# Split weights that begin at places of their own in SBUF: one change to a two-layer encoder kernel

## The chip, the cores and the metric

The kernel runs on one core of one Trainium2 chip. The metric is the device time of one execution in microseconds (us), lower is better. A core has five engines that run side by side: PE (TensorE, matrix products; its weight loads are shown apart, as PEld), ACT (ScalarE), DVE (VectorE), POOL (GpSimd) and SP (SyncE, here only a queue for DMA transfers). SBUF, the working memory, has 128 partitions; PSUM takes the products.

## What is computed

The reference is an encoder of two layers on a sequence of 256 tokens with 1024 features, in float32. Each layer is a mixer and a feed-forward part:

```python
def mixer_sublayer(x, ...):
    proj = rms_norm(x, n1) @ w_in_l                  # 1024 -> 2560
    out_a = neighbourhood_attention(...)             # 4 heads
    out_d = dilated_window_attention(...)            # 6 heads
    out_c = gqa_block_attention(...)                 # 6 heads on 2 key heads
    mix = concat(rms_norm(out_a), rms_norm(out_d), rms_norm(out_c))
    return x + mix @ w_out_l                         # 1024 -> 1024

def channel_sublayer(x, n2, w_gu, cw, cb, w_dn):
    g, u = split(rms_norm(x, n2) @ w_gu)             # 1024 -> 2 x 2816
    g = depthwise_conv_centred(g, cw, cb)            # three taps along the tokens
    return x + (gelu(g) * u) @ w_dn                  # 2816 -> 1024
```

Nearly all the arithmetic is in the four products with weights (w_in, w_out, w_gate_up, w_down).

## The kernel before, in words

**Split products.** PE reads float32 operands in a form of reduced precision (float32r), so each float32 value is split in two: hi is the value cast to float32r, lo is the rest. A product is made of three: hi by hi, hi by lo and lo by hi (`mm3`, lines 708 to 711). The activations are split once into tiles (hT, mixT_hi and mixT_lo, ch and cl), the weights on the way in.

**Units.** The weights come in units of at most 2048 float32 values per partition (8192 bytes), listed by `units_of` in the order of use. A layer has 51 (`PER_LAYER`): 12 units of the input projection, 6 of the output projection (together `LAST_OUT` = 18), then 33 of the feed-forward part in the order of `FFN`. There the 11 steps each have a gate unit G, an up unit U and a down unit D. For each unit, `load` (line 644) starts a DMA transfer into one of four raw buffers, and `split` (line 676) makes hi and lo from it piece by piece: ACT casts raw into hi (the CAST of `wp_hi<-wp_raw` in the profile), DVE subtracts (the TENSOR_TENSOR of `wp_lo<-wp_raw,wp_hi`). hi and lo have two buffers each, `wp_hi` and `wp_lo`, so two units are split at any time: PE reads one while ACT and DVE write the other. `unit` (line 697) hands out the next one.

**Which operand a unit is.** In the projections and in the down products the split weights are the moving operand, streamed through PE in 256, 384 or 512 columns, and the activations are the stationary one, 128 columns loaded by a LDWEIGHTS ahead of each matmul. In the gate and up products (`half_up`, line 1337) it is the other way round: the weights are loaded, 128 columns at a time, and h2 (in the buffer hT) is streamed. A gate or up unit is two halves of 8 wide matmuls (512 columns, hi of the weights by hi and lo of h2 at once) and 8 narrow ones (256 columns, lo of the weights). A down unit is 24 matmuls of 512 columns.

**Kept units.** The 6 output-projection units of the second layer are loaded and split early, during the first layer's feed-forward part, and kept in DRAM (`keep`, line 628). Four of them come back into hi and lo by DMA from POOL's queue (the `nc.gpsimd.dma_start` in `split`); the last two have tiles of their own (kc and qc).

**Where tiles lie.** Tiles stand one behind the other in SBUF in the order of their allocation. Two tiles ahead of the wp pool, `minus_half` and `few_out`, are wider than what is used of them, and the raw, hi and lo buffers, hT, ch, cl, mixT and the other operands of matmuls begin on multiples of 512 bytes within the partition. Exceptions are const_x, which lies 384 bytes past one, and every second slice of heads in the value tiles const_v, 256 bytes past one.

**The order of the work.** Calls on `nc` are recorded as operations, and `Plan.order` (line 323) sets their order by a model of the engines' times; the table `PLACES` (line 229) shifts some by hand. `emit` (line 467) writes them out, so all instructions carry its line 472 in the profile, and groups are told apart by their tiles.

Of the kernel before, what the change touches and what calls it, by code (L numbers as in the profile page):

```python
# [12 lines left out]
F32R = mybir.dt.float32r  # L13
# [5 lines left out]
P = 128  # L19
S = 256  # L20
NT = S // P
D = 1024
# [14 lines left out]
UNIT = 2048  # L37
# [4 lines left out]
RAWS, PARTS, AHEAD, CHUNK = 4, 2, 2, 512  # L42
# [34 lines left out]
FFN = [("G", 0), ("U", 0)]  # L77
# [161 lines left out]
class Plan:  # L239
# [5 lines left out]
    def pool(self, real, name, bufs, space=bass.MemoryType.SB):  # L245
        return PlanPool(self, real, name, bufs, space)
# [271 lines left out]
def encoder_kernel(  # L518
# [26 lines left out]
    wp = pool("wp", 3)  # L545
# [78 lines left out]
    PER_LAYER = len(views) // DEPTH  # L624
    LAST_OUT = PER_LAYER - len(FFN)
# [18 lines left out]
    def load(i):  # L644
# [28 lines left out]
                nc.sync.dma_start(rv[:, c:e], v[:, c:e])  # L673
        raws.append(raw)

    def split(i):
        v = views[i]
        a, b = v.shape[1], v.shape[2]
        n = a * b
        raw = raws[i]  # L680
        if isinstance(raw, list):
            parts.append(raw)
            return
        hi = wp.tile([P, UNIT], F32R, tag="hi", name=f"hi{i}", bufs=PARTS)
        lo = wp.tile([P, UNIT], F32R, tag="lo", name=f"lo{i}", bufs=PARTS)
        h = b if i < 2 else b * max(1, CHUNK // b)
        if i in kept:
            for d, z in zip(kept[i], (hi, lo)):
                nc.gpsimd.dma_start(z[:, :n], d)
        for c in range(0, n if i not in kept else 0, h):  # L690
            e = min(c + h, n)
            nc.scalar.copy(hi[:, c:e], raw[:, c:e])
            nc.vector.tensor_tensor(lo[:, c:e], raw[:, c:e], hi[:, c:e].bitcast(F32), op=ALU.subtract)
        r = lambda z: z[:, :n].rearrange("p (a b) -> p a b", b=b)
        parts.append((r(hi), r(lo)))

    def unit():

        i = taken[0]
        taken[0] += 1  # L700
        with nc.later(SPLIT_LATER):
            while len(raws) < min(i + AHEAD + RAWS - PARTS, len(views)):
                load(len(raws))
            while len(parts) < min(i + AHEAD, len(views)):
                split(len(parts))
        return parts[i]
# [182 lines left out]
    for l in range(DEPTH):  # L889
# [3 lines left out]
        if l == 0:  # L893
            gains_T(0, 1)
            split(0)
# [656 lines left out]
```

## Time and profile before

| | |
|---|---|
| time, median of 3 runs | 605.8 us (604.55 to 605.87) |
| time of the profiled execution | 605.52 us |
| its span, first to last instruction | 603.7 us |
| PE busy | 598.0 us (99%) |
| PEld busy | 526.5 us (87%) |
| DVE busy | 485.0 us (80%) |
| ACT busy | 428.6 us (71%) |
| POOL busy | 81.0 us (13%) |
| DMA | 121.44 MB, 201 GB/s over the span |

Of the 605.52 us, 1.8 lie around the span. Busy time is the union of an engine's instructions. A matmul's recorded duration includes a modelled tail that overlaps the next one, so PE's pace is read from starts: the length of a piece of the chain of waits divided by its matmuls. The mean granted clock of PE over the span is 1.000 of full speed.

### The profile page before, as it was taken

What the parts mean: (1) busy time and instruction counts of PE and PEld (TensorE: products, weight loads), DVE (VectorE), ACT (ScalarE), POOL (GpSimd) and SP (SyncE); (2) the same over time, 40 slices, a digit from 0 to 9 for tenths busy, and PEclk for the clock granted to TensorE, in tenths of its full rate; (3) what the DMA queues carried; (4) which work ended last, traced back from release to release, by engine and by line L of the source; (5) the groups of instructions that cost most, each with busy time, mean ns of one, the idle gap of its engine ahead of it and who ended that gap; (6) DMA issues with size and microseconds to landing.
All of it is one profiled execution on the core that took longest, in us unless ns stands there. A gap on an engine that the chain in (4) does not pass through costs nothing.

```text
span 603.7 us, 9899 instructions
## 1 busy us (share of the span) xinstructions
PE 598.0 (99%) x3496; PEld 526.5 (87%) x3496; DVE 485.0 (80%) x995; ACT 428.6 (71%) x1065; POOL 81.0 (13%) x130
## 2 busy tenths in 40 slices
PE   8999999999999999999999999999999999999997
PEld 7999898888888888888899989888888888888886
DVE  4899988997788988888777898777977777777775
ACT  6889999696566767666688899676766556665661
POOL 2733030102400000000023214421000000000000
PEclk9999999999999999999999999999999999999999
DMA  8993313567588898989454726844465556555601
GB/s 281 292 334 108 106 36 108 181 202 241 174 239 295 280 347 301 331 291 318 153 148 157 254 71 244 280 177 140 140 208 203 171 186 210 175 178 206 197 12 69
DMA packets 85217, 121.44 MB, mean 201 GB/s; under 512 B 9880, under 2 KB 69880, under 8 KB 85168
## 3 DMA queue, kind: packets, MB, share of 16 engines
q1 hardware_dynamic: 82896, 112.17, 55.9%
q0 software_dynamic: 1728, 8.39, 4.1%
q8 instruction: 27, 0.44, 0.3%
q10 hardware_dynamic: 544, 0.26, 0.2%
q14 instruction: 22, 0.18, 0.1%
HBM read 110.93 MB, written 9.88 MB: 200 GB/s over the span
## 4 chain that ended last, share of the span: by engine, by line
PE 97%; ACT 1%; DVE 1%; POOL 0%; issue 0%; DVEq 0%; POOLq 0%
PE psw_w L472 53%; PE psa_a L472 44%; ACT act_s2k L472 0%; POOL small_rstd L472 0%; ACT act_z L472 0%; DVE act_z L472 0%; ACT act_hT L472 0%; DVE wp_lo L472 0%; DVE act_sw L472 0%; POOL small_ms L472 0%; DVE const_x L472 0%; DVE act_qo L472 0%; ACT wp_hi L472 0%; POOL const_warm L472 0%; DVEq L472 0%
## 5 line engine op out<-in xcount | busy, mean ns | idle before, releaser
L472 DVE TENSOR_TENSOR wp_lo<-wp_raw,wp_hi 128x512 fp32r<-128x512 f32 (+2 forms) x332 | 231.4, 731 | 57.2 <-ACT wp_hi L472 40.3
L472 ACT CAST wp_hi<-wp_raw 128x512 fp32r<-128x512 f32 (+2 forms) x332 | 203.0, 663 | 21.6 <-PE psw_w L472 10.1
L472 PE MATMUL psw_w<-act_hT,wp_hi 128*128 128x512 f32 x704 | 179.8, 393 | 0.0
L472 PEld LDWEIGHTS psw_w<-act_hT,wp_hi 128*128 128x128 f32 x704 | 127.8, 189 | 24.2 <-DVE act_hT L472 0.6
L472 PE MATMUL psa_a<-wp_hi,act_hT 128*128 128x384 f32 (+2 forms) x448 | 112.9, 332 | 0.7 <-ACT wp_hi L472 0.7
L472 PEld LDWEIGHTS psw_w<-act_hT,wp_lo 128*128 128x128 f32 x704 | 97.7, 190 | 6.7
L472 PE MATMUL psw_w<-act_hT,wp_lo 128*128 128x256 f32 x704 | 102.2, 282 | 0.0
L472 PEld LDWEIGHTS psa_a<-wp_hi,act_hT 128*128 128x128 f32 x448 | 78.4, 189 | 3.3 <-ACT wp_hi L472 0.9
L472 PE MATMUL psa_a<-wp_lo,act_hT 128*128 128x384 f32 (+2 forms) x224 | 74.4, 334 | 0.1
L472 ACT COPY act_s2k<-psw_w 128x256 f32<-128x256 f32 x88 | 32.4, 372 | 59.4 <-PE psw_w L472 58.9
L472 PE MATMUL psa_a<-wp_lo,act_ch 128*128 128x512 f32 (+1 forms) x176 | 68.3, 388 | 0.0
L472 PE MATMUL psa_a<-wp_hi,act_ch 128*128 128x512 f32 x176 | 68.2, 388 | 0.0
L472 PE MATMUL psa_a<-wp_hi,act_cl 128*128 128x512 f32 (+1 forms) x176 | 67.5, 387 | 0.0
L472 DVE TENSOR_TENSOR act_s2k<-psw_w,act_s2k 128x256 f32<-128x256 f32 x88 | 36.6, 421 | 12.8 <-ACT act_s2k L472 12.0
L472 PEld LDWEIGHTS psa_a<-wp_lo,act_hT 128*128 128x128 f32 x224 | 42.3, 189 | 2.4 <-DVE wp_lo L472 1.1
L472 PEld LDWEIGHTS psa_a<-wp_hi,act_cl 128*128 128x128 f32 x176 | 33.1, 188 | 6.8
L472 PEld LDWEIGHTS psa_a<-wp_hi,act_ch 128*128 128x128 f32 x176 | 33.1, 188 | 6.3
L472 PEld LDWEIGHTS psa_a<-wp_lo,act_ch 128*128 128x128 f32 x176 | 33.1, 188 | 6.0
L472 DVE SCALAR_TENSOR_TENSOR act_s2k<-act_s2k,act_cw,act_s2k 128x255 f32<-128x255 f32 x88 | 36.8, 477 | 1.4 <-ACT act_s2k L472 1.3
L472 ACT ACTIVATE act_s2k<-act_s2k 128x512 f32<-128x512 f32 x22 | 13.9, 632 | 30.3 <-DVE act_s2k L472 30.2
L472 ACT ACTIVATE act_s2k<-act_s2k,act_cw 128x256 f32<-128x256 f32 x44 | 24.1, 596 | 15.3 <-DVE act_s2k L472 15.3
L472 POOL TENSOR_TENSOR small_rstd<-small_ms,const_mh 128x6 f32<-128x6 f32 (+2 forms) x26 | 30.9, 1188 | 14.2 <-DVE small_ms L472 12.6
(132 smaller groups left out, 792.0 us busy)
## 6 DMA issues: line engine op xcount, KB each, us to landing
wp_raw<-in_w_gate_up_dram SPq DMA_DIRECT2D x44, 1024.0 KB, 4.9
wp_raw<-in_w_down_dram SPq DMA_DIRECT2D x22, 1024.0 KB, 7.2
wp_raw<-in_w_in_dram SPq DMA_DIRECT2D x14, 768.0 KB, 5.2
wp_raw<-in_w_in_dram SPq DMA_DIRECT2D x8, 1024.0 KB, 6.8
wp_raw<-in_w_out_dram SPq DMA_DIRECT2D x8, 768.0 KB, 9.3
dram_khi<-act_mixT_hi SPq DMA_DIRECT2D x4, 768.0 KB, 3.6
dram_klo<-act_mixT_lo SPq DMA_DIRECT2D x4, 768.0 KB, 8.3
wp_lo<-dram_klo POOLq DMA_DIRECT2D x4, 768.0 KB, 4.7
```

The source lines that it names most:

```text
L472: getattr(o.engine.real, o.method)(*map(real, o.args), **{k: real(v) for k, v in o.kw.items()})
```

## The change: a place for each unit

Each hi and lo tile grows from 8192 to 8704 bytes per partition, and the unit begins in it at an offset that a table gives, in bytes, for hi and for lo. The table has a row for the 12 units of the input projection (the 6 of the output projection take its first six pairs again), one for the steps of the gate and up units, and one for the steps of the down units. The same offsets hold in both layers. All are multiples of 16. Everything that writes or reads the unit (cast, subtraction, kept transfer, matmul) uses the shifted place. The instructions on every engine and their order are the same as before. Later tiles move up by up to 2048 bytes in all, in steps of 512, and so keep their remainder.

```diff
+    APART = {
+        "w": [(0, 64), (64, 0), (32, 32), (192, 192), (448, 448), (256, 256), (0, 192), (320, 64), (16, 16), (96, 96), (480, 480), (352, 352)],
+        "G": [(0, 64), (16, 16), (48, 48), (64, 96), (96, 80), (128, 32), (256, 192), (288, 224), (352, 320), (416, 448), (480, 480)],
+        "D": [(0, 0), (64, 64), (0, 64), (64, 0), (192, 192), (192, 0), (320, 320), (448, 448), (256, 256), (0, 256), (16, 16)],
+    }
+
+    def places_of(i):
+
+        n = i % PER_LAYER - LAST_OUT
+        if n < 0:
+            return APART["w"][(n + LAST_OUT) % 12]
+        kind, s = FFN[n]
+        return APART["D" if kind == "D" else "G"][s]
+
     def split(i):
...
-        hi = wp.tile([P, UNIT], F32R, tag="hi", name=f"hi{i}", bufs=PARTS)
-        lo = wp.tile([P, UNIT], F32R, tag="lo", name=f"lo{i}", bufs=PARTS)
+        hi, lo = (
+            wp.tile([P, UNIT + 128], F32R, tag=g, name=f"{g}{i}", bufs=PARTS)[:, at // 4 : at // 4 + UNIT]
+            for g, at in zip(("hi", "lo"), places_of(i))
+        )
```

## The prediction

> **What bounds the kernel now.** I read the page's busy times first, then its chain of waits, then who waits for whom on PE, and then the chain again inside one stretch of the feed-forward part.
>
> ```profile
> span 603.7 us, 9899 instructions
> PE 598.0 (99%) x3496; PEld 526.5 (87%) x3496; DVE 485.0 (80%) x995; ACT 428.6 (71%) x1065; POOL 81.0 (13%) x130
> PE 97%; ACT 1%; DVE 1%; POOL 0%; issue 0%; DVEq 0%; POOLq 0%
> PE psw_w L472 <- POOL const_warm L472: 1.0, 1, 1.0
> PE psa_a L472 <- ACT wp_hi L472: 0.7, 1, 0.7
> ```
>
> PE is busy for 598.0 of 603.7 us, 97% of the chain that ends last is PE itself, and the waits on PE add up to 1.7 us. So the time is the sum of 3496 start-to-start distances on PE. No other engine sets it: what a change does to the time is what it does to those distances, unless it makes PE wait for something that it doesn't wait for now.
>
> The next rows are the chain between 138 and 172 us (start, length, matmuls in the piece). A piece `psa_a x24` is one down unit (24 matmuls of 512 columns); a piece `psw_w x64` is an up unit and the next gate unit (32 matmuls of 512 columns on hi, 32 of 256 on lo).
>
> ```profile
> 138.31 5.47 PE psa_a L472 x24
> 143.77 11.15 PE psw_w L472 x64
> 154.92 5.47 PE psa_a L472 x24
> 160.38 11.15 PE psw_w L472 x64
> ```
>
> The pieces repeat to 0.01 us, although they use other buffers and other steps. From them: 5.47 / 24 = 227.9 ns per 512-column matmul. In the piece of 64, 32 x 227.9 ns = 7.29 us, which leaves 3.86 us for the 32 narrow ones, 120.5 ns each. The 256 columns between the two cost 107.4 ns, 0.42 ns a column; 512 columns at that rate are 214.8 ns, and 13.1 ns are left over in each matmul whatever its width. This constant is the only thing in a matmul that a change of address could touch, since width, count and order stay.
>
> How far a single matmul strays from its usual length is in the rows of the tiles wp_hi and wp_lo (duration min/median/max, count):
>
> ```profile
> L472 PEld LDWEIGHTS psw_w<-act_hT,wp_hi x704: 186/188/192, 120.1 to 587.1; 128*128 128x128 f32 x176
> L472 PE MATMUL psw_w<-act_hT,wp_hi x704: 387/389/497, 120.1 to 587.3; 128*128 128x512 f32 x176
> L472 PE MATMUL psw_w<-act_hT,wp_lo x704: 274/283/287, 120.4 to 588.4; 128*128 128x256 f32 x176
> L472 PE MATMUL psa_a<-wp_hi,act_mixT_hi x56: 387/393/503, 84.0 to 408.3; 128*128 128x512 f32 x56
> L472 PE MATMUL psa_a<-wp_lo,act_mixT_hi x56: 387/395/506, 84.3 to 408.6; 128*128 128x512 f32 x56
> ```
>
> These durations contain a modelled tail, so only their differences count. A 512-column matmul is 387 ns at least, 389 in the middle, and 393 to 395 in the middle of the output projection; a 256-column one on lo is 274 at least and 283 in the middle, 287 at most. The weight load varies from 186 to 192. So a matmul of one width does vary by some ns, always with hi and lo on multiples of 512 bytes: something in how the weight load and the streaming meet moves it, and it is not excluded that the place of the operands is part of that.
>
> **The change, part by part.** *What is moved.* Every matmul that reads a split unit from the wp pool counts. Counted in the code there are 1408 in the gates and ups, 672 in the projections, 540 in the downs and 168 in the output projections, 2788 in all. By the table of places 328 of these still read from an offset of zero; 2460 read from another (912 of 256 columns, 304 of 384, 1244 of 512). No instruction is added, removed or reordered, and no semaphore changes.
>
> *What 0.3% means.* A measurement of this kernel can tell about 0.3%, 1.8 us, from no change. Over 2460 matmuls that is 0.74 ns each: the whole question is whether the constant of 13.1 ns moves by 0.7 ns on the average over the places.
>
> *Price on PE.* The trace of before holds two groups whose weights do not begin on a multiple of 512 bytes. Adding up the sizes of the tiles in the order of allocation, const_x lies 384 bytes past one, and in const_v every second slice of heads begins 256 past one. Beside them stand transposes from aligned tiles and the aligned narrow matmuls:
>
> ```profile
> L472 PE MATMUL psw_w<-const_ident,const_x x64: 270/272/421, 4.7 to 417.7; 128*128 128x128 f32 x64
> L472 PE MATMUL psw_w<-const_ident,act_z x60: 270/272/273, 28.6 to 379.4; 128*128 128x128 f32 x60
> L472 PE MATMUL psw_w<-act_ch,const_v x128: 274/282/387, 55.0 to 404.8; 128*128 128x256 f32 x128
> ```
>
> At 384 bytes the median is 272, as it is for z at zero; with half of the weights at 256 it is 282, against 283 for the aligned lo matmuls. So at these two places nothing shows. Both are multiples of 128 bytes; 254 of the 2460 moved matmuls sit on such places, and for the other 2206 (16, 32, 48, 64, 80, 96 and so on) the trace has no row. I take the value of the nearest rows, zero, and bound the rest by the strays of the aligned groups. Downwards: if every moved matmul ran at its group's least, 912 x 9 ns + 1244 x 2 ns + 304 x 2 ns = 11.3 us less. Upwards: if every moved matmul lost the 4 ns that lie between 389 and 393 (and between 283 and 287), 2460 x 4 = 9.8 us more. A gain is not excluded, as the 274 shows.
>
> *Splits on ACT and DVE.* They now write hi and lo at the new places. What covers them, in two of the stretches above:
>
> ```profile
> 138.31:143.78 5.47, 5.47 (x25) 4.51 (x25) 4.85 (x10) 3.04 (x6) 0.00 (x0) 1.00 0.80 237
> 143.77:154.92 11.15, 11.15 (x66) 9.83 (x65) 8.21 (x12) 6.98 (x13) 8.08 (x12) 1.00 0.62 215
> ```
>
> After the length, the columns are the busy times of PE, PEld, DVE, ACT and POOL. Over a step of 16.62 us DVE is busy for 13.06, so its work would have to grow by 27% before it could set the pace. That DVE minds the place much is not seen: the convolution's operands are shifted by 4 bytes, and they cost per element what the aligned splits cost.
>
> ```profile
> L472 DVE TENSOR_TENSOR wp_lo<-wp_raw,wp_hi 128x512 fp32r<-128x512 f32 x224 | 144.8, 685 | 25.9 <-ACT wp_hi L472 24.3 <-PE psw_w L472 1.3
> L472 DVE TENSOR_TENSOR wp_lo<-wp_raw,wp_hi 128x1024 fp32r<-128x1024 f32 x44 | 53.6, 1223 | 26.0 <-PE psw_w L472 15.4 <-ACT wp_hi L472 10.6
> L472 DVE SCALAR_TENSOR_TENSOR act_s2k<-act_s2k,act_cw,act_s2k 128x255 f32<-128x255 f32 x88 | 36.8, 477 | 1.4 <-ACT act_s2k L472 1.3
> L472 DVE SCALAR_TENSOR_TENSOR const_x<-psa_a,small_rstd,const_x 128x512 f32<-128x512 f32 x24 | 17.7, 743 | 1.2 <-PE psa_a L472 0.9
> ```
>
> Splits: (1223 - 685) / 512 = 1.05 ns an element. The other form: (743 - 477) / 257 = 1.04. Price on the path: zero; if the cover went, PE would wait for wp_lo.
>
> *Kept units.* Four units of the second layer reach hi and lo by DMA from POOL's queue, also to the new places. The tightest one:
>
> ```profile
> 388.95 0.57 POOL L472 DMA_DIRECT2D wp_hi<-dram_khi  x1
> 394.96 0.62 PE L472 MATMUL psa_a<-wp_hi,act_mixT_hi 128*128 128x512 f32 x2
> wp_hi<-dram_khi POOLq DMA_DIRECT2D x4, 768.0 KB, 5.9
> ```
>
> Issued at 388.95 and landing after 5.9 us, at 394.85, it is used at 394.96. There is 0.1 us of cover. If odd places made that transfer a fifth longer, PE would wait 1.1 us once; a shorter one brings nothing, since PE waits for none now. I take zero and keep 1.1 us for the range, inside 0.3%.
>
> *Sum.* 0 on PE, 0 for splits, 0 for kept units, against the profiled execution's 603.7 us of span and 605.5 us in all, which is 0.3 us under the median of the three runs. The forecast is the median, 605.8 us.
>
> **The rivals.** *Slower: the streams meet more often.* The place is PE's: the weight load and the moving operand, both on multiples of 512 today, settle into the same pattern in each unit (pieces equal to 0.01 us). Shifted against each other by 16 to 480 bytes they settle elsewhere, and the pace becomes that of the output projection, 4 ns more, where matmuls of the three kinds follow each other less regularly. It decides from 0.74 ns on average, a fifth of the 2460 at 4 ns. For: the 4 to 6 ns between groups, and the constant of 13.1 ns, which looks like such a meeting. Against: 256 and 384 bytes, where nothing shows. With half of the moved ones hit, 2460 x 4 / 2 = 4.9 us more, 610.7 us; with all, 615.6.
>
> [...]
>
> *Faster: the streams meet less.* The 274 ns of a narrow matmul against 283 says that part of the constant can vanish. If half of the moved matmuls reach their group's least, 11.3 / 2 = 5.6 us less, 600.2 us; with all, 594.5. For: equal starts could be the worst case rather than the best. Against: the least occurs in before with equal starts too, so it comes from the neighbours in the queue and needs no shift, and a mixture of places would hit good and bad ones alike.
>
> [...]
>
> *The change does not do what it says.* The places are in the operands' offsets and the tiles grow by 512 bytes, so all later tiles stay on the same remainder of 512. This can only fail through a sub-512 effect that does not exist, which is the forecast.
>
> **How the numbers follow.** No change within 0.3%: 0.42, because the only rows off 512 show nothing, and because good and bad places cancel in a mixture. Slower: 0.32, ahead of faster at 0.26, because the aligned state sits close to the least of its group (389 against 387) and farther from the upper strays (393 to 395), at least for the wide matmuls. The range goes from midway between 600.2 and 594.5 to midway between 610.7 and 615.6: 597.4 to 613.2 us, which leaves out about a quarter of each rival, 0.15 in all. The likeliest case's own range is 604.0 to 607.6.
>
> **What would show it.** In the chain after, each step has its own place, so the pieces of 5.47 and 11.15 us can be read one by one against the table. I am right if all stay within 0.03 us. I am wrong if they differ from step to step: 0.1 us on a piece of 24 is 4 ns a matmul. The first down unit, at offset zero, must stay at 5.47 in any case. PE's waits should stay under 3 us, the split medians where they are; a wait of PE for wp_lo or for a DMA would show a lost cover.

## The result and the profile after

| | before | after |
|---|---|---|
| median of 4 runs each, side by side | 605.49 us (604.55 to 605.87) | 608.88 us (608.62 to 610.04) |
| profiled execution | 605.52 us | 608.62 us |
| its span | 603.7 us | 606.9 us |

The ratio is 1.0062, with a 95% interval of 1.0044 to 1.008: slower by 0.6%. The forecast of no change was wrong, though the time lies in the range.

First the page of after (span, busy times, chain by engine), then PE's waits.

```profile
span 606.9 us, 9908 instructions
PE 600.2 (99%) x3496; PEld 524.4 (86%) x3496; DVE 484.7 (80%) x995; ACT 428.5 (71%) x1065; POOL 80.5 (13%) x130
PE 96%; ACT 1%; DMA 1%; DVE 1%; POOL 0%; SPq 0%; issue 0%
```

```profile
PE psw_w L472 <- POOL const_warm L472: 1.0, 1, 1.0
PE psa_a L472 <- ACT act_hT L472: 0.8, 1, 0.8
PE psa_a L472 <- ACT wp_hi L472: 0.7, 1, 0.7
```

PE is still nearly the whole chain (96%), and its waits sum to 2.5 us, 0.8 more than before. PE's busy time grew by 2.2 us, DVE's and ACT's did not grow. So most of the loss lies inside PE's own work. (The total of instructions differs by nine, all of the sequencers; the five counts of the second row are those of before.)

Where in it, the chain of after shows (start, length, matmuls in the piece). A piece of 64 is the up unit of a step and the gate unit of the next one.

```profile
138.80 5.46 PE psa_a L472 x24
144.27 11.13 PE psw_w L472 x64
155.40 5.60 PE psa_a L472 x24
161.01 11.21 PE psw_w L472 x64
...
222.67 5.63 PE psa_a L472 x24
228.30 11.17 PE psw_w L472 x64
239.47 5.50 PE psa_a L472 x24
...
272.90 5.47 PE psa_a L472 x24
...
435.49 5.46 PE psa_a L472 x24
440.95 11.13 PE psw_w L472 x64
452.09 5.60 PE psa_a L472 x24
457.69 11.21 PE psw_w L472 x64
```

Before, every down unit took 5.47 us (one at 191.57 us 5.44) and every piece of 64 took 11.15. Now each step has a length of its own, and it repeats in the second layer to 0.02 us (the pieces from 435.49 on are those from 138.80 on again). Only step 3 differs by more, 5.58 and 5.55 us: in the first layer its down unit starts in the middle of an up unit. The down units at (0, 0) and at (256, 256), at 138.80 and 272.90, keep the old length; (64, 64) costs 5.60, (192, 0) 5.63, (320, 320) 5.50. A gain on one side and a loss on the other are in the rows of the tiles wp_hi and wp_lo (duration min/median/max):

```profile
L472 PE MATMUL psw_w<-act_hT,wp_hi x704: 387/394/502, 120.5 to 590.5; 128*128 128x512 f32 x176
L472 PE MATMUL psw_w<-act_hT,wp_lo x704: 274/280/286, 120.9 to 591.5; 128*128 128x256 f32 x176
```

The wide matmul's median rises from 389 to 394, the narrow one's falls from 283 to 280. Added up over the starts of the 3496 matmuls in the trace, by what a matmul reads, after minus before in us:

| wide gate and up | narrow gate and up | down | projections | output projection | all others | sum |
|---|---|---|---|---|---|---|
| +1.98 | -1.15 | +1.68 | +0.95 | +0.25 | -0.57 | +3.14 |

The projections and "all others" hold waits that move from run to run: the kernel with grown tiles and all places at zero (below) has +0.74 and -0.64 there.

The other engines' rows that answer to those of before, the subtraction that makes lo, and the tightest kept transfer:

```profile
L472 DVE TENSOR_TENSOR wp_lo<-wp_raw,wp_hi 128x512 fp32r<-128x512 f32 x224 | 144.7, 685 | 27.8 <-ACT wp_hi L472 25.9 <-PE psw_w L472 1.8
L472 DVE TENSOR_TENSOR wp_lo<-wp_raw,wp_hi 128x1024 fp32r<-128x1024 f32 x44 | 53.6, 1223 | 26.6 <-PE psw_w L472 17.0 <-ACT wp_hi L472 9.6
wp_hi<-dram_khi POOLq DMA_DIRECT2D x4, 768.0 KB, 6.0
```

685 and 1223 ns are the numbers of before to the last digit, and the transfer lands after 6.0 us instead of 5.9, with no wait of PE on it.

### The profile page after: what moved, and what is told of

Read it like the earlier page. It is cut to its first block, busy times and chain, and to the rows that moved or that the text cites. A ratio compares the mean times of both kernels' runs of the same rounds, so it can differ in the third digit from the quotient of the medians.

```text
span 606.9 us, 9908 instructions
## 1 busy us (share of the span) xinstructions
PE 600.2 (99%) x3496; PEld 524.4 (86%) x3496; DVE 484.7 (80%) x995; ACT 428.5 (71%) x1065; POOL 80.5 (13%) x130
## 4 chain that ended last, share of the span: by engine, by line
PE 96%; ACT 1%; DMA 1%; DVE 1%; POOL 0%; SPq 0%; issue 0%
PE psw_w L472 52%; PE psa_a L472 45%; DMA const_x<-in_x_dram 1%; ACT act_s2k L472 0%; SPq L472 0%; POOL small_rstd L472 0%; ACT act_z L472 0%; ACT act_hT L472 0%; DVE act_z L472 0%; POOL small_ms L472 0%; DVE const_x L472 0%; DVE wp_lo L472 0%; DVE act_qo L472 0%; ACT wp_hi L472 0%; ACT act_qo L472 0%
## 5 line engine op out<-in xcount | busy, mean ns | idle before, releaser
L472 PE MATMUL psw_w<-act_hT,wp_hi 128*128 128x512 f32 x704 | 181.8, 395 | 0.0
```

The source lines that it names most:

```text
L472: getattr(o.engine.real, o.method)(*map(real, o.args), **{k: real(v) for k, v in o.kw.items()})
```

## The experiments

**The theory and its rivals.** The theory, after the trace of after: a matmul's cost depends on the distance between the places of its two operands (loaded and streamed). That the rhythm so set carries over into the following matmuls was added after the third kernel. The rivals: growing the tiles and moving the later ones does it; each operand's own place does it; what ACT and DVE write at the same time does it; a place has a fixed price, whatever came before.

**Is it the growth of the tiles, or an operand's own place?** The first kernel is the changed one with all places at zero (of the table, one row is shown here; w and G are changed likewise). The second also moves everything behind `few_out` by 64 bytes together, so the operands of the products with weights begin 64 past a multiple of 512, at unchanged distances (the identity of the transposes and the value tiles lie ahead of `few_out` and stay).

```diff
-        "D": [(0, 0), (64, 64), (0, 64), (64, 0), (192, 192), (192, 0), (320, 320), (448, 448), (256, 256), (0, 256), (16, 16)],
+        "D": [(0, 0)] * 11,
```

```diff
-    few_out = const.tile([P, 496], F32, tag="fo", name="few_out")[:, :1]
+    few_out = const.tile([P, 512], F32, tag="fo", name="few_out")[:, :1]
```

Grown tiles alone:

> The changed kernel with every place set to 0: the tiles have grown by 512 bytes and all later tiles have moved up, but each unit begins on a multiple of 512 again. Both theories (A: the distance between the loaded weights and the moving operand sets the pace; B: a unit's own distance from a multiple of 512 sets it) expect the time of before, 605.5 us, and chain pieces of 5.47 and 11.15 us. If the growth of the tiles is what costs, it stays at 608.9.

Everything at 64 together:

> All places 0, but one tile ahead of the wp pool is 64 bytes longer, so raw, hi, lo and all operands of the large products begin 64 bytes past a multiple of 512 together; the distance between the two operands of a matmul stays 0. A (distance): 605.5 us, a down unit 5.47 us, a narrow matmul group 0.95 us, as before. B (own place): as e3_units64, about 610.5 us, a down unit 5.60 us.

Measured: 605.58 us, ratio 0.999 (0.9979 to 1.0), and 605.89 us, ratio 0.9996 (0.9983 to 1.0009). The chain with grown tiles, and then with everything at 64:

```profile
138.31 5.47 PE psa_a L472 x24
143.78 11.15 PE psw_w L472 x64
154.92 5.47 PE psa_a L472 x24
```

```profile
138.40 5.47 PE psa_a L472 x24
143.87 11.15 PE psw_w L472 x64
155.02 5.47 PE psa_a L472 x24
```

The lengths are those of before. Neither the growth nor a shift of all operands by 64 costs anything. So a place that both operands share is not what counts here (5.47 and 11.15 us at 64 as at 0); what is left of these is the distance between the operands.

**One distance for all.** The third kernel puts every unit of the table at (64, 64); the fourth leaves the units at zero and shifts the streamed activations, hT and h2, by 64.

```diff
+        "D": [(64, 64)] * 11,
```

```diff
-        h2 = act.tile([P, KD, 2, S], F32R, tag="hT", name=f"h2{l}", bufs=1)
+        h2 = act.tile([P, KD * 2 * S + 128], F32R, tag="hT", name=f"h2{l}", bufs=1)[:, 16 : 16 + KD * 2 * S].rearrange(
+            "p (k a s) -> p k a s", k=KD, a=2, s=S
+        )
```

All units at 64:

> Every unit, hi and lo, at 64 bytes past a multiple of 512; the activations stay at 0. Both theories: slower than before. A down unit 5.60 us as at its step 1 in the changed kernel (0.135 us x 22 = 2.9 us), a gate or up half 13 ns more (24 more on hi, 11 less on lo, x 88 = 1.1 us), the projections about 1.5 ns a matmul more (1.3 us): about 610.8 us.

The activations at 64:

> All units at 0; only the buffer of the normed activations (hT, h2) begins 64 bytes past a multiple of 512. In gates and ups it is the moving operand, so the weights lie 448 past it, counted modulo 512. A (distance): the narrow groups become those of the unit at 448, 0.914 us instead of 0.953, the wide ones about 1.86 instead of 1.84, so a piece of 64 about 11.11 us; total of gates and ups about 1.4 us less, the projections about as in e3. B (own place of a unit): pieces of 64 stay at 11.15, all of it at 605.5 us; if the moving operand's own place counts, 32 x 5.6 ns more on a piece of 64, 11.33 us, and about 4 us more in all.

Measured: 605.31 us, ratio 0.9986 (0.9973 to 0.9999), and 604.13 us, ratio 0.9967 (0.9953 to 0.9981). The chains:

```profile
138.21 5.49 PE psa_a L472 x24
143.70 11.10 PE psw_w L472 x64
154.80 5.49 PE psa_a L472 x24
```

```profile
137.37 5.46 PE psa_a L472 x24
142.84 11.09 PE psw_w L472 x64
153.93 5.46 PE psa_a L472 x24
```

The first expectation missed by 5.5 us. Of the second, the length of a piece came out (11.09 us for 11.11) and the gain on gates and ups nearly (1.34 us for 1.4), but not its split between wide and narrow matmuls. With all units at 64 a down unit takes 5.49 us, while the same places took 5.60 in after; so a place does not have one price. The groups' sums show two effects that nearly cancel: wide gate and up matmuls +2.35 us, narrow ones -3.32, downs +0.45. A half of a gate or up unit (8 matmuls), median of the halves, in ns:

| | 8 wide | 8 narrow |
|---|---|---|
| before, (0, 0) | 1841 | 953 |
| units at (64, 64) | 1862 | 912 |
| activations at 64 | 1835 | 944 |

With the activations at 64 the distance has the other sign, and the numbers differ: the medians are near those of weights at 192 and 448 in the tables below, 64 short of a multiple of 256. They hide two rhythms, though: in nearly every gate unit the first half takes 1834 and 907 ns and the second 1828 and 944, at one distance.

**Does the rhythm carry over?** The fifth kernel has all down units at (64, 64) behind gates of different places: step 0 to 8 behind a gate at 0, 0, 64, 64, 48, 48, 64, (0, 64), (64, 0). It has a table of its own for the ups.

```diff
+        "G": [(0, 0), (0, 0), (0, 0), (64, 64), (64, 64), (48, 48), (48, 48), (64, 64), (0, 64), (64, 0), (0, 0)],
+        "U": [(0, 0), (0, 0), (64, 64), (0, 0), (64, 64), (48, 48), (64, 64), (48, 48), (0, 64), (64, 0), (0, 0)],
+        "D": [(64, 64)] * 11,
```

> All down units at (64, 64), where a unit took 5.602 us in the changed kernel and 5.494 us when every unit stood at 64. Gate and up units have places of their own per step, so that each of the downs 0 to 8 follows a gate unit at one place (the last matmuls before it) while an up unit is written at another. Theory C (the rhythm carries over from the matmuls before): downs 0 and 1 (after a gate at 0) agree, downs 2, 3 and 6 (after a gate at 64) are 5.494 us, downs 4 and 5 (after a gate at 48) 5.602. Theory W (what ACT and DVE write meanwhile sets it): downs 1, 3 and 5 (up unit at 64) agree at 5.494, downs 4 and 6 (up unit at 48) at 5.602. Plain theory A (the distance inside the unit alone): all nine agree. Total about 605 to 608 us.

Measured, one run: 609.91 us. The down units of the second layer, steps 0 to 8, in the chain:

```profile
436.93 5.60 PE psa_a L472 x24
...
453.71 5.60 PE psa_a L472 x24
...
470.45 5.49 PE psa_a L472 x24
...
487.09 5.49 PE psa_a L472 x24
...
503.75 5.50 PE psa_a L472 x24
...
520.49 5.60 PE psa_a L472 x24
...
537.23 5.49 PE psa_a L472 x24
...
553.91 5.51 PE psa_a L472 x24
...
570.60 5.60 PE psa_a L472 x24
```

The same 24 matmuls at the same places take 5.49 to 5.51 us behind a gate at 64 or (0, 64), and 5.60 behind a gate at 0 or (64, 0). So it goes with the place of lo, which the last eight matmuls of the gate load. The rhythm lasts through the unit: from start to start the matmuls of step 2 repeat in threes (225 to 227, 229 or 230, 231 or 232 ns), and those of step 1 take 233 or 234, but for the first and the last. Behind a gate at 48, step 4 takes 5.60 in the first layer and 5.50 in the second, and step 5 takes 5.60 in both: there the gate's place alone does not settle it. What enters a unit decides up to 0.11 us of it, 4.6 ns a matmul. A fixed price of a place falls. So does a price set by what ACT and DVE write meanwhile: while a down unit runs they split the next up unit, which lay at 0 in steps 0 and 2 and at 64 in steps 1 and 3, and the lengths follow the gate, 5.60 in the first two steps and 5.49 in steps 2 and 3. (The time, expected at 605 to 608 us, also holds 2.0 us of PE's waits for kept units in this one run.)

**Which distances are good?** In the sixth kernel hi stays at 0 and lo takes a place by step, in the seventh lo stays at 64 and hi takes a place by step (gates and ups; everything else at zero).

```diff
+        "G": [(0, 64), (0, 16), (0, 32), (0, 96), (0, 128), (0, 192), (0, 256), (0, 320), (0, 384), (0, 448), (0, 480)],
```

```diff
+        "G": [(480, 64), (16, 64), (32, 64), (48, 64), (96, 64), (128, 64), (192, 64), (256, 64), (320, 64), (384, 64), (448, 64)],
```

hi at 0:

> Projections and downs at 0; gates and ups with hi at 0 and lo at 64, 16, 32, 96, 128, 192, 256, 320, 384, 448, 480 by step. If the two distances count each for itself: wide groups 1.84 us at every step, narrow ones 0.94 at most places, 0.914 at 448. If the rhythm carries over from group to group, the wide groups change with the place of lo. At 256 both as before (1.841 and 0.953). Total 603 to 606 us.

lo at 64:

> Projections and downs at 0; gates and ups with lo at 64 and hi at 480, 16, 32, 48, 96, 128, 192, 256, 320, 384, 448 by step. If each distance counts for itself, the narrow groups are equal at all steps (0.912 us, as with every unit at 64) and the wide ones 1.84 at 16 and 256, 1.86 elsewhere; if the rhythm carries over, the narrow ones change with the place of hi. Total 603 to 607 us.

Measured, one run each: 604.83 and 604.48 us, beside 605.58 for before. The halves in ns, without the first half behind a down unit or behind the start:

| place of lo, hi at 0 | narrow half | place of hi, lo at 64 | wide half | narrow half |
|---|---|---|---|---|
| 64 / 320 | 943 / 943 | 320 | 1862 to 1867 | 911 to 923 |
| 128 / 384 | 962 / 962 | 128 / 384 | 1857 to 1858, both | 918 to 923, both |
| 192 / 448 | 941 to 947, both | 192 / 448 | 1835 / 1835 | 912 / 912 |
| 256 (0 before) | 952 (953) | 256 (0 in after) | 1837 to 1840 (1838) | 942 (942) |
| 16, 32, 96 | 940 to 950 | 16 | 1865 | 943 |
| 480 | 932 to 936 | 32, 48, 96, 480 | 1854 to 1879 | 910 to 946 |

Places that differ by 256 read alike in every pair (0 and 256, 64 and 320, 128 and 384, 192 and 448): in these runs the period is 256 bytes. (320 with lo at 64 has no partner here; it lies near the 1862 and 912 of all units at 64.) And a narrow half at 64 costs 943 behind a wide half at 0 and 912 behind one at 192: the carry-over again, inside one unit. The wide halves show it too: with hi at 0 at every step, they take from about 1824 to 1860 ns as the place of lo changes. The sum of wide and narrow in these two kernels is least at (192, 64) and (448, 64), 2747 ns against 2794 before.

**The parts of the change alone.** The eighth kernel keeps only the table's row for the downs, the last one only the row for the gates and ups; all else is at zero.

```diff
+        "w": [(0, 0)] * 12,
+        "G": [(0, 0)] * 11,
+        "D": [(0, 0), (64, 64), (0, 64), (64, 0), (192, 192), (192, 0), (320, 320), (448, 448), (256, 256), (0, 256), (16, 16)],
```

Downs only:

> The changed kernel's places for the down units alone; gates, ups and projections at 0. If the parts add up, the downs cost what they cost in the changed kernel, 1.7 us: 607.2 us. If the rhythm carries over from the gate unit ahead (C), the down pieces differ from the changed kernel's at the same places, and the total is between 605.5 and 607.5.

Gates and ups only:

> The changed kernel's places for gates and ups alone, downs and projections at 0. By the changed kernel's own sums (wide groups 2.0 us more, narrow ones 1.15 less) 0.8 us more than before, 606.4 us. With the downs at 0 the up units start from another rhythm than in the changed kernel, so up to 0.5 us less than that.

Measured: downs only 608.05 us, ratio 1.0041 (1.0027 to 1.0056); gates and ups only 606.12, ratio 1.0009 (1.0 to 1.0019). The chain with the downs only (steps 5, 6 and 7), and PE's waits in it:

```profile
222.15 5.62 PE psa_a L472 x24
...
238.95 5.60 PE psa_a L472 x24
...
255.74 5.61 PE psa_a L472 x24
```

```profile
PE psa_a L472 <- DMA wp_lo<-dram_klo: 1.5, 1, 1.5
...
PE psa_a L472 <- DMA wp_hi<-dram_khi: 0.7, 1, 0.7
```

Step 6 at (320, 320) takes 5.60 us behind a gate at 0; in after, behind its gate at (288, 224), it took 5.50. At 320, as at 64, the same place has the two lengths, as the period and the carry-over have it. Downs alone cost 2.47 us by the medians, more than the 1.7 of adding up and above the 605.5 to 607.5 us expected with the carry-over. In the trace 2.0 us of it are the down matmuls and 0.4 the wide ones behind them: a first half behind a down unit takes 1813 ns there after a down at (0, 0), and up to 1853 after a moved one. The waits for the kept units lie on top in this execution, which took 610.63 us, 2.6 above its median. The places of the kept units are zero here, so these 2.2 us are not the price of a place: the 0.1 us of cover is gone for another reason. Gates alone cost 0.47 us: +1.97 us on wide matmuls and -1.15 on narrow ones, as in after. Together 2.9 of the 3.4 us; the rest lies within the intervals, and the places of the projections were not tried alone.

**A choice of distances.** The ninth kernel puts all gates and ups at (192, 64), the rest at zero; the tenth adds the two units of the input projection with 256 columns at (192, 192).

```diff
+        "G": [(192, 64)] * 11,
```

```diff
+        "w": [(0, 0)] * 8 + [(192, 192), (0, 0), (0, 0), (192, 192)],
```

The pair:

> Every gate and up unit at (192, 64), all other units at 0. If distance and what went before set the rhythm, each half of a unit takes 2.747 us as at this pair in e7_lo64, against 2.794: 0.047 us x 88 = 4.1 us less, 601.5 us, and a piece of 64 is 4 x 2.747 = 10.99 us. If the short halves of that run were due to its mixture of places, the pieces go back to 11.1 and the time to about 605 us.

With the two units of the projection:

> As e9_pair, and the two 256-column units of the projections at (192, 192), the distance at which their matmuls stood in e4_hT64 (114 ns instead of 120). 192 matmuls x 5.3 ns = 1.0 us less than e9_pair: 600.5 us. If the distance does not carry over from moved activations to moved weights, no change from e9_pair.

Measured: 602.44 us, ratio 0.9945 (0.9933 to 0.9958), and 601.87 us, ratio 0.9934 (0.9922 to 0.9947). The chain with the pair, and PE's wait there for a kept unit; then the narrow matmuls of the tenth:

```profile
137.64 5.46 PE psa_a L472 x24
143.10 11.00 PE psw_w L472 x64
154.10 5.46 PE psa_a L472 x24
159.56 11.00 PE psw_w L472 x64
```

```profile
PE psa_a L472 <- DMA wp_hi<-dram_khi: 1.0, 1, 1.0
```

```profile
L472 PE MATMUL psw_w<-act_hT,wp_lo x704: 276/276/284, 120.0 to 584.9; 128*128 128x256 f32 x176
```

Every piece of 64 falls from 11.15 to 11.00 us, and narrow matmuls take 276 ns instead of 283. The gain on them is 3.25 us (ninth) and 3.16 (tenth), with nothing lost on wide ones (+0.02 and +0.06). Both kernels gain a little less than expected. Halves behind a down unit were at 2766 ns before and only fall to 2754, which fits the carry-over from the down unit. In the tenth, the projection's matmuls of 256 columns fall from 120 to 117 ns and not to the 114 that the activations at 64 gave. Counted modulo 256 the distance is the same in both, so the distance alone does not settle the cost; whether the rest is the carry-over was not tried. The tenth beats both kernels: 601.87 against 605.65 and 608.88 us.

## Why the prediction was wrong, point by point

**What bounds the kernel: right.** The time is the sum of PE's distances. After, PE is 96% of the chain with 2.5 us of waits, and the loss of 3.2 us of span is the +3.14 us of distances. Its split of a piece of 64 was a little off: by the starts of before, a wide matmul of a half takes 230 ns on the average and a narrow one 119 (1841 and 953 for 8), where it worked with 227.9 and 120.5.

**The price on PE: the step that failed**, "I take the value of the nearest rows, zero". The two rows could not show the effect. 256 bytes is one period, so it reads as zero (a wide and narrow half 1837 to 1840 and 942 ns at 256, 1838 and 942 at 0). 384 reads as 128, and at 128 a narrow half differs by 9 ns in 8 matmuls, about 1 ns each; the row at 384 is of transposes, with medians given to 1 ns. (That the period holds for transposes too is assumed.) The prediction noted that both were multiples of 128 and that 2206 moved matmuls had no row, and still gave the missing rows the value of these two. What was measured in its place: +1.28 ns on the average of 2460 moved matmuls (3.14 us), where 0.74 was the line.

**The bounds: held for the sum, not for each place.** Down units lose up to 0.16 us in 24 matmuls, 6.7 ns each, where 4 ns was taken as the most; a wide half loses up to 38 ns in 8, 4.8 ns each (1879 against 1841). A narrow one gains up to 47 ns, 5.9 ns each (906 against 953), where 9 was the bound. That the time lies in the range is in part luck: the bounds on losses were too low, and the two signs partly cancel.

**"Good and bad places cancel in a mixture": failed as an argument for zero.** They cancel in part only: +1.98 and +1.68 us on matmuls of 512 columns stand against -1.15 on the narrow ones. The aligned rhythm of the wide ones, 226 or 227 ns inside a unit of before (1813 ns for 8), is the least that the traces of before and after show for 8 matmuls of 512 columns in a row, so another distance has more to lose there than to gain.

**The slower rival: right that the starts settle elsewhere, its price of 4.9 us for half of the moved ones came out at 3.1.** The starts of the matmuls do settle into other patterns with the distance between what is loaded and what is streamed (a wide half 1841 ns at (0, 0), 1862 with all units at 64). That the two streams meet in the chip was a reading of the rows; no run shows whether or where they do. Its condition, one pattern per place, was too simple: the pattern also depends on what came before (5.49 or 5.60 us). **The faster rival** is true for the narrow gate and up matmuls of the same kernel (-1.15 us). For the whole kernel it came true by 0.5% where one chosen distance stood in all gates and ups (602.44 us). The mixtures of the sixth and seventh kernel gained 0.25 and 0.63 us on gates and ups in one trace each, so a mixture need not lose.

**The constant of 13.1 ns: part of it does move.** With all units at 64 a narrow half takes 912 ns instead of 953, 5 ns a matmul. The best narrow rhythm, 113 ns for 256 columns (906 for 8), leaves about 6 ns by the prediction's estimate of 0.42 ns a column, which comes from the pieces of before.

**Splits at zero: right** (685 and 1223 ns, unchanged). **Kept units at zero: right for this change, but the cover is as thin as said (0.1 us).** Kernels with these units at place zero wait 0.7 to 1.5 us for them (downs only, the pair) or not at all (gates only, the tenth), so a wait there says nothing about a place. In the two that wait, the transfers to hi take 6.9 and 6.7 us from issue to landing (median), where the other two have 6.0 and 5.9. What slows them was not tried.

**What would show it: this worked.** The pieces differ from step to step by up to 0.16 us, (0, 0) stays, and the waits stay under 3 us.

## What to carry to other kernels

Where PE bounds a kernel and a LDWEIGHTS stands ahead of every matmul, the distance between the start of the loaded and that of the streamed operand is worth a try, at least with float32r operands as here: one distance for a whole run of like matmuls gained most (3.2 us on gates and ups, against 0.25 and 0.63 us for two mixtures and a loss of 0.8 us for that of the change). Read it from the start-to-start distance of matmuls inside one piece, not from the kernel's time, where gains and losses cancel. A row at one remainder says nothing of another until the period is known.

## What was not expected of the hardware

- In these runs the cost of a float32r matmul goes with the distance of its operands' starts, with a period of 256 bytes (a narrow half with hi at 0 takes 943 ns at 64 and at 320, 962 at 128 and at 384, 941 to 947 at 192 and at 448, and 952 at 256 where before has 953 at 0), and not with a place that both share (everything at 64: 605.89 us, pieces of 5.47 and 11.15 us as before).
- Matmuls of the same shape at the same places ran in different lasting rhythms, depending on what ran before: a down unit at (64, 64) took 5.49 to 5.51 or 5.60 us, a narrow half at 64 took 943 ns behind a wide half at 0 and 912 behind one at 192.
- The alignment on 512 bytes that the kernel before has is good for the 512-column matmuls of the gates and ups (1841 ns for 8; 1835 with the chosen pair) and poor for the 256-column ones (953 for 8; 912 with the pair, 906 at the least seen).
